# Alternating the array's halves in the half-array products of two recurrences

## The chip, the cores and the metric

The kernel runs on one core of a Trainium2 chip. The metric is device time in microseconds; the kernel before takes 3214.45 us (median of three runs, 3214.08 to 3216.48). TensorE is called PE below, with its weight loads as PEld; VectorE is DVE, ScalarE ACT, GpSimd POOL, SyncE SP.

## The reference

One block of a hybrid model over 2048 tokens of width 1024, in front of which 256 context tokens are scanned. Four branches (a gated convolution, a recurrence with a decay per channel, a Fourier mix, a recurrence with one decay per head) are gated and summed, and a hierarchical mixture of 32 experts follows. Both recurrences are this scan, run in both directions over four heads of 64 channels:

```python
def step(state, inp):
    qc, kc, vc, gc = inp
    cum = jnp.cumsum(gc, axis=-2)
    rel = cum[..., :, None, :] - cum[..., None, :, :]
    decay = jnp.exp(jnp.where(incl, rel, -jnp.inf))
    ...
    out = (jnp.einsum('bhts,bhse->bhte', scores, vc)
           + jnp.einsum('bhtd,bhde->bhte', qc * jnp.exp(cum), state))
    last = cum[..., -1:, :]
    state = (jnp.exp(last[..., 0, :])[..., None] * state
             + jnp.einsum('bhsd,bhse->bhde', kc * jnp.exp(last - cum), vc))
    return state, out
```

## The kernel before

The kernel is written in the tile framework: the order of the instructions on each engine is not the order of the code but is planned when the kernel is built, from the dependencies, the pools' buffers and assumed durations. Each engine then takes its instructions strictly in that order.

Stages, by the trace: modulation and norms, then projections (to 570 us); the first recurrence `hgrn` (576 to 908 us) beside the second half's projections; the second recurrence `ssm` (its preparation from 908, its products from 985 to 1266 us) beside the gates of the second half of the tokens; the Fourier branch (to about 1400 us) beside the rest of these gates; the gated sum of the branches (1465 to 2025 us); router and experts (to 3100 us); the weighted sum. Projections and gates are products of 128x128 weights with 512 or 256 columns in three parts (L1339 to L1341, tile `ps_mm`). They depend on no recurrence and are planned between the recurrences' instructions; below they are the fillers.

`hgrn` goes over four segments of 512 tokens, and two pairs of heads in each: eight passes. The two heads of a pair lie on partitions 0 to 63 and 64 to 127, so a product that contracts over one head's channels uses half of the array's rows. A pass computes scores without decay (L123) and then those of seven levels with blocks of 1, 2, 4 up to 64 tokens (L137). Such a group is four products of the first head and then four of the second, each head's in a bank `pa` of its own (tag `sc`, two banks), from which ACT (L124) or DVE (`copy_predicated`, L139) takes them into `ST`. DVE then multiplies `QP` by the level's decay (L143), the moving operand of the next group, and `K2` (L144), from which ACT makes the next level's `km` (L132). After the last level the states are advanced (L54, L59, L67) and the outputs `po` are summed in one bank (L156, L158, L159): for each of four chunks and two heads one product of values and scores (all 128 rows, 64 columns of the array), and two with the states that enter from the left and the right (64 rows, 64 columns). A square on ACT (L161), a product with ones (L163), a root on ACT (L165) and a reciprocal on DVE (L166) norm them.

`ssm` computes a state per chunk of 64 tokens in `d_state` (L311: two products on half of the rows, chunks alternate between the halves), backward over all chunks and then forward; per segment scores of two groups on half of the rows each (L393); and per 128 tokens and head one product with the scores (L413) and one for each of two chunks with the entering state (L417), 64 columns of the array each, heads alternating between the column halves.

All these products are fp32, and the profile shows each as two matmul records.

Of the kernel before, what the change touches and what calls it, by code (L numbers as in the profile page):

```python
# [21 lines left out]
def mix(base, off, n, w, B):  # L22
    """halves of blocks of 2B: the left ones of part 0, the right ones of part 1 (parts w apart)"""
    return ap_of(base, off, [[2 * B, n // (2 * B)], [w + B, 2], [1, B]])


def hgrn(G, tc, khm, FT, KT, QT, GT, V, YT, bufs=1):
    """FT, KT [2 dir, 2 panel][128, TA]; QT, GT [2 panel][128, T]; V [18][128, 256]; YT [2][128, T]"""
    nc = tc.nc
    SEG = 512  # L30
    with tc.tile_pool(reuse_waits="tile", name="hst", bufs=1) as st, tc.tile_pool(reuse_waits="tile", name="hw", bufs=bufs) as wp, \
# [17 lines left out]
        def states(ks, tot, v, hp, n, cs, S, src, dst):  # L49
            """ks [128, n] decayed keys, tot [128, n/128]; cs: chunks in order; S[:, hp, dst(c)] from S[:, hp, src(c)]"""  # L50
# [38 lines left out]
        # context: the final states of both directions start the scans  # L89
# [3 lines left out]
        # backward states: SB[c] enters chunk c from the right  # L93
# [5 lines left out]
        for sg in range(4):  # L99
# [3 lines left out]
            for hp in range(2):  # L103
# [13 lines left out]
                nc.vector.tensor_add(km, K2[:, 0], K2[:, 1])  # L117
                for h in range(2):
                    r = slice(h * 64, h * 64 + 64)
                    pa = G.psum("sc")  # L120
                    for c in range(4):
                        s = slice(c * 128, c * 128 + 128)
                        nc.tensor.matmul(pa[:, s], km[r, s], q[r, s], start=True, stop=True)  # L123
                    nc.scalar.copy(ST[:, h].rearrange("p c t -> p (c t)"), pa)  # L124
# [3 lines left out]
                while B < 128:  # L128
# [3 lines left out]
                    nc.scalar.copy(kmv, mix(K2, 0, n, n, B))  # L132
                    for h in range(2):
                        r = slice(h * 64, h * 64 + 64)
                        pa = G.psum("sc")
                        for c in range(4):
                            nc.tensor.matmul(pa[:, c * 128:c * 128 + 128], km[r, c * 128:c * 128 + 128],  # L137
                                             mix(QP[r], c * 128, 128, n, B), start=True, stop=True)
                        nc.vector.copy_predicated(ST[:, h], hmask[:, lev].unsqueeze(1).to_broadcast([128, 4, 128]),  # L139
                                                  pa.rearrange("p (c t) -> p c t", t=128))  # L140
# [11 lines left out]
                for c in range(4):  # L152
                    s = slice(c * 128, c * 128 + 128)
                    for h in range(2):
                        r = slice(h * 64, h * 64 + 64)
                        nc.tensor.matmul(po[r, s], v[:, c, hp * 128 + h * 64:hp * 128 + h * 64 + 64], ST[:, h, c, :],  # L156
                                         start=True, stop=False)
                        nc.tensor.matmul(po[r, s], SF[r, hp, c0 + c], QP[r, 1, s], start=False, stop=False)  # L158
                        nc.tensor.matmul(po[r, s], SB[r, hp, c0 + c], QP[r, 0, s], start=False, stop=True)  # L159
# [15 lines left out]
def ssm(G, tc, dtr, XR, ZT, XC, XB, cumD, ecumD, elD, SBd, YT):  # L175
    """dtr [128, 18, 8] raw steps (tokens on partitions); XR [4][128, TA] xs0 xs1 b c before the convolution; ZT [2][128, T];
    scratch in DRAM: XC [4][128, TA], XB [18][128, 384], cumD [2, 8, 18, 64], ecumD [8, TA], elD [8, 36], SBd [32][64, 256]"""
    nc = tc.nc
    NCH = TA // 64
    with tc.tile_pool(reuse_waits="tile", name="sst", bufs=1) as st:  # L180
        # ---- steps and cumulated logs
# [85 lines left out]
        with tc.tile_pool(reuse_waits="tile", name="sw", bufs=1) as wp, tc.tile_pool(reuse_waits="tile", name="ssp", bufs=2) as sp:  # L267
            # ---- convolution
# [37 lines left out]
            def d_state(xb, xw, c, d):  # L306
                i, r = c // 2, slice((c % 2) * 64, (c % 2) * 64 + 64)
                pd = G.psum("sc")
                o = slice(d * 64, d * 64 + 64)
                for g in range(2):  # L310
                    nc.tensor.matmul(pd[o, g * 128:g * 128 + 128], xb[r, i, 256 + g * 64:320 + g * 64],  # L311
                                     xw[r, i, g * 128:g * 128 + 128], start=True, stop=True)
                return pd[o, 0:256]
# [10 lines left out]
            # ---- context: final states; then the backward states of all chunks  # L324
            S = None
            xb, xw = seg_in(T, TC, 1)
            for c in (3, 2, 1, 0):
                S2 = sp.tile([128, 256], F32, name="Sb", bufs=3)
                step(S2, S, 32 + c, d_state(xb, xw, c, 1), 1)
                S = S2  # L330
            for sg in (3, 2, 1, 0):
                xb, xw = seg_in(sg * 512, 512, 1)
                for c in range(7, -1, -1):
                    ch = sg * 8 + c
                    nc.sync.dma_start(SBd[ch], S[64:128])
                    if ch:
                        S2 = sp.tile([128, 256], F32, name="Sb", bufs=3)
                        step(S2, S, ch, d_state(xb, xw, c, 1), 1)
                        S = S2
            S = None  # L340
            xb, xw = seg_in(T, TC, 0)
            for c in range(4):
                S2 = sp.tile([128, 256], F32, name="Sf", bufs=4)
                step(S2, S, 32 + c, d_state(xb, xw, c, 0), 0)
                S = S2
# [5 lines left out]
            for sg in range(4):  # L351
# [35 lines left out]
                PT = PTs[0]  # L387
                for g in range(2):
                    pa = G.psum("sc")
                    r = slice(g * 64, g * 64 + 64)  # L390
                    for i in range(4):
                        s = slice(i * 128, i * 128 + 128)
                        nc.tensor.matmul(pa[:, s], bT[r, s], cT[r, s], start=True, stop=True)  # L393
                    pv = pa.rearrange("p (i c t) -> p i c t", c=2, t=64)
# [5 lines left out]
                for i in range(4):  # L400
                    Sc = []
                    for c2 in range(2):
# [4 lines left out]
                        if ch < 31:  # L407
                            S2 = sp.tile([128, 256], F32, name="Sf", bufs=4)
                            step(S2, S, ch, d_state(xb, xw, c, 0), 0)
                            S = S2  # L410
                    for h in range(4):
                        g, o = h // 2, slice((h % 2) * 64, (h % 2) * 64 + 64)
                        nc.tensor.matmul(py[g][o, i * 128:i * 128 + 128], xb[:, i, h * 64:h * 64 + 64], PT[:, h, i],  # L413
                                         start=True, stop=False)
                        for c2 in range(2):
                            a = i * 128 + c2 * 64
                            nc.tensor.matmul(py[g][o, a:a + 64], Sc[c2][:, h * 64:h * 64 + 64], ec[:, h, a:a + 64],  # L417
                                             start=False, stop=c2 == 1)
# [19 lines left out]
def rnd12(a):  # L438
    """nearest float32 with 11 explicit mantissa bits"""
# [5 lines left out]
def dft_consts():  # L445
    """time: cos, sin of 2 pi t t'/2048, t' odd (512), 2 mod 4 (256), 4 mod 8 and 0 mod 8 (128, 130 with 1024);
    channels: cos, sin of 2 pi c c'/64 with the ortho scale, two groups on the diagonal"""
    def cs(n, tp):
        ph = (np.arange(n)[:, None] * np.asarray(tp)[None, :]) % 2048
        a = ph * (2 * np.pi / 2048)  # L450
        return np.stack([np.cos(a), np.sin(a)], 1).astype(np.float32)   # [t, 2, t']
    def split(a):
        hi = rnd12(a)
        return np.stack([hi, rnd12(a - hi)], 1)                      # [t, hi/lo, 2, t']
# [13 lines left out]
def fft(G, tc, U, YT, A):  # L468
    """U [16][128, 256] tokens on partitions; YT [2][128, T]"""
# [76 lines left out]
CAP = 2048          # a token picks an expert at most once  # L546
NSLOT = 2           # blocks per expert in the straight part: 128 tokens, then 64
FIT = 192
NONE = 1 << 20      # no assignment
RAW, PARTS = 9, 15  # panels of experts' weights on chip: as they come, in two parts  # L550
AHEAD = 6           # tiles loaded ahead in the last step
OVB = 32            # bound on the blocks beyond those


def ffn(tc, G, A, out, bcast, rsqrt, split, mm3, MT, MR, X1, FR, YB, mid):
# [9 lines left out]
    hl = rp.tile([128, 2, 2, N], BF, name="hl")             # (token + k T) / 64 + 1, and the rest  # L565
# [8 lines left out]
    def assign(dst_a, dst_r, v, t):  # L574
        """assignments and rows of tokens from table values v (-64: none)"""
# [6 lines left out]
    # ---------------- output projection, second norm, routing  # L582
    # its operands lie where the mixer's did
    wring = mid.wring
    with tc.tile_pool(reuse_waits="tile", name="wo", bufs=1, side="right") as wop, \
# [6 lines left out]
        wo = [y0, [[t[:, 2 * k:2 * k + 2] for t in w1] for k in range(4)]]      # columns, pair of chunks, part  # L592
# [78 lines left out]
        def route(p0, i0, M, lg):  # L671
            """the tiles of tokens i0 .. i0 + M, p0 tiles were before: weights, ranks among an expert's tokens, table"""
# [5 lines left out]
            def first_max(src, k, n):  # L678
                """maximum and the first place that has it, as 0/1"""
# [59 lines left out]
            # weights: the group's probability times the softmax over the two  # L739
# [12 lines left out]
        # in the order in which they come; a tile's logits stand between the next ones' products  # L752
# [3 lines left out]
        at, tiles = {}, {}              # what follows a half of a tile's products  # L756
# [29 lines left out]
    # ---------------- experts  # L786
# [4 lines left out]
    def unit(src, q=nc.sync, eng=nc.vector):  # L791
        """the two parts of a panel of an expert's weights"""
# [6 lines left out]
    class InTurn:  # L799
        """panels that are fetched when their turn comes, one at a time"""  # L800
# [762 lines left out]
```

## Time and profile before

| what | value |
|---|---|
| runs, median (lowest to highest) | 3214.45 us (3214.08 to 3216.48) |
| the profiled execution: span from the first to the last instruction | 3204.4 us |
| median less that span | 10.0 us |
| PE busy | 2935.5 us, 92% |
| weight loads busy | 2333.6 us, 73% |
| DVE busy | 1903.9 us, 59% |
| ACT busy | 1239.4 us, 39% |
| POOL busy | 856.6 us, 27% |
| mean granted TensorE clock | 0.962 |

No separate time of the profiled execution is given beside its span; 10 us is what the median of the runs has more. Busy time is the union of an engine's instructions; matmuls are pipelined and their ends are modelled, so two records can overlap in time without running beside each other, and the distance from one start to the next tells more than a duration. A granted clock of 1.00 is 2.4 GHz, 0.50 is 1.2 GHz. In a timeline, successive instructions of one line, tile and shape are merged into one row with their count.

### The profile page before, as it was taken

The numbers are of one execution on the slowest core, as the hardware profiler recorded it, in microseconds if no ns is written. First come the engines' busy times: TensorE is split into PE (matmuls) and PEld (weight loads), VectorE is DVE, ScalarE is ACT, GpSimd is POOL, SyncE is SP. The second block draws the span as 40 slices with busy tenths as digits, with TensorE's granted clock in tenths as the row PEclk, the third lists the DMA queues.
The fourth block names the chain that finished last, engine by engine and source line by source line (L and its number), as shares of the span: only waits on it lengthen the run. The fifth ranks groups of instructions, "written<-read, shape, count | busy, mean of one in ns | idle before, by whom it ended". The sixth has DMA issues, their size and how long they took to land. (4 is left out here: it accounts for less than half of the span.)

```text
span 3204.4 us, 40958 instructions
## 1 busy us (share of the span) xinstructions
PE 2935.5 (92%) x14805; PEld 2333.6 (73%) x14805; DVE 1903.9 (59%) x2956; ACT 1239.4 (39%) x1751; POOL 856.6 (27%) x589
## 2 busy tenths in 40 slices
PE   7998999999988999899999999999699999999950
PEld 4887887787766677677777777877577887778740
DVE  4524125877776568523334334566888768776758
ACT  5411132322236122132213212222577667776744
POOL 3300010000013112013334333000345544544435
PEclk8999999999998999999999999999799999999975
DMA  7636244422128476866336334432787888888884
GB/s 299 231 122 190 85 158 156 134 75 84 53 78 262 145 190 189 266 228 218 127 127 207 125 126 153 159 127 104 270 309 281 276 275 316 307 298 281 284 316 178
DMA packets 241878, 625.50 MB, mean 195 GB/s; under 512 B 27832, under 2 KB 75608, under 8 KB 237944
## 3 DMA queue, kind: packets, MB, share of 16 engines
q1 hardware_dynamic: 208784, 513.34, 47.1%
q0 software_dynamic: 32880, 109.38, 10.2%
q8 instruction: 126, 2.06, 0.3%
q14 instruction: 88, 0.72, 0.1%
HBM read 501.47 MB, written 129.27 MB: 197 GB/s over the span
## 5 line engine op out<-in xcount | busy, mean ns | idle before, releaser
L1196 DVE TENSOR_TENSOR mlo<-mraw,mhi 128x1024 fp32r<-128x1024 f32 x318 | 388.6, 1275 | 3.3 <-ACT mhi L1195 3.1
L1195 ACT CAST mhi<-mraw 128x1024 fp32r<-128x1024 f32 x384 | 387.0, 1053 | 7.1 <-DMA mraw<-e 6.8
L1339 PE MATMUL ps_mm<-hb1h,wlo 128*128 128x512 f32 x800 | 319.3, 399 | 10.3 <-ACT ev L1490 10.2
L1340 PE MATMUL ps_mm<-hb1l,whi 128*128 128x512 f32 x800 | 318.6, 398 | 0.0
L1341 PE MATMUL ps_mm<-hb1h,whi 128*128 128x512 f32 x800 | 318.3, 398 | 0.0
L1490 ACT ACTIVATE ev<-ps_mm 128x512 f32<-128x512 f32 x128 | 76.3, 598 | 594.4 <-PE ps_mm L1341 501.8
L1196 DVE TENSOR_TENSOR wlo<-wraw,whi 128x1024 fp32r<-128x1024 f32 x164 | 215.1, 1320 | 134.2 <-ACT whi L1195 132.1
L1339 PE MATMUL ps_mm<-hb0h,wlo 128*128 128x512 f32 x672 | 269.4, 401 | 6.3 <-DVE wlo L1196 6.3
L1340 PE MATMUL ps_mm<-hb0l,whi 128*128 128x512 f32 x672 | 269.3, 401 | 0.0
L1341 PE MATMUL ps_mm<-hb0h,whi 128*128 128x512 f32 x672 | 268.4, 399 | 0.0
L1540 POOL TENSOR_TENSOR macc<-macc,ev 128x512 f32<-128x512 f32 x96 | 167.3, 1743 | 309.5 <-DVE ev L1539 306.6
L1196 POOL TENSOR_TENSOR mlo<-mraw,mhi 128x1024 fp32r<-128x1024 f32 x66 | 209.9, 3196 | 136.4 <-ACT mhi L1195 125.8
L1195 ACT CAST whi<-wraw 128x1024 fp32r<-128x1024 f32 x176 | 182.2, 1045 | 152.8 <-PE ps_mm L1341 65.5
L1539 DVE TENSOR_TENSOR ev<-ev,ps_tr 128x512 f32<-128x512 f32 x96 | 65.8, 687 | 248.3 <-PE ps_tr L1341 244.0
L1339 PE MATMUL ps_mm<-mhi,xl 128*128 128x512 f32 x512 | 204.8, 400 | 0.1
L831 POOL DMA_INDIRECT xg<-d_FR,idx x48 | 129.3, 2695 | 270.8 <-PE ps_tr L848 221.6
L1341 PE MATMUL ps_mm<-mhi,xh 128*128 128x512 f32 x512 | 201.1, 393 | 0.3
L1340 PE MATMUL ps_mm<-mlo,xh 128*128 128x512 f32 x512 | 200.8, 392 | 0.3
L1339 PEld LDWEIGHTS ps_mm<-hb1h,wlo 128*128 128x128 f32 x800 | 151.5, 189 | 44.9 <-ACT ev L1490 11.0
L1340 PEld LDWEIGHTS ps_mm<-hb1l,whi 128*128 128x128 f32 x800 | 151.4, 189 | 33.5 <-issue 3.0
L1341 PEld LDWEIGHTS ps_mm<-hb1h,whi 128*128 128x128 f32 x800 | 151.2, 189 | 33.8 <-issue 2.7
L1339 PEld LDWEIGHTS ps_mm<-hb0h,wlo 128*128 128x128 f32 x672 | 127.8, 190 | 35.2 <-DVE wlo L1196 7.1
(605 smaller groups left out, 6618.4 us busy)
## 6 DMA issues: line engine op xcount, KB each, us to landing
mraw<-e SPq DMA_DIRECT2D x372, 512.0 KB
wraw<-wg SPq DMA_DIRECT2D x80, 512.0 KB
wraw<-wt SPq DMA_DIRECT2D x40, 512.0 KB
aw<-adaw SPq DMA_DIRECT2D x64, 256.0 KB
d_GS<-ev SPq DMA_DIRECT2D x64, 256.0 KB
ev<-d_GS POOLq DMA_DIRECT2D x64, 256.0 KB, 4.7
yk<-d_YB SPq DMA_DIRECT2D x32, 512.0 KB
wraw<-wg POOLq DMA_DIRECT2D x24, 512.0 KB, 4.4
```

Source lines behind the costliest of these rows:

```text
L831: nc.gpsimd.indirect_dma_start(out=xg, out_offset=None, in_=FR, in_offset=bass.IndirectOffsetOnAxis(ap=idx_ap, axis=0), bounds_check=T - 1 ...
L1195: nc.scalar.copy(hi, raw)
L1196: eng.tensor_sub(lo, raw, hi.bitcast(F32))
L1339: nc.tensor.matmul(ps, wl, xh, start=start and n == 0, stop=False)
L1340: nc.tensor.matmul(ps, wh, xl, start=False, stop=False)
L1341: nc.tensor.matmul(ps, wh, xh, start=False, stop=stop and n == len(ks) - 1)
L1490: nc.scalar.activation(g, ps, AF.Sigmoid)
L1539: nc.vector.tensor_mul(g, g, ps)
L1540: nc.gpsimd.tensor_add(acc, acc, g)
```

## The change

In both recurrences the products on half of the array are written so that the halves take turns, and each half has its own bank:

- the groups L123 and L137 of `hgrn` take both banks first and then go chunk by chunk, one head after the other; the two copies out of the banks follow the eight products;
- `po` is summed in three runs of one shape each: the entering states of the first head, then values and scores of both heads in turn, then the entering states of the second head; the flags that start a sum move with it;
- `d_state` becomes `d_states`, which makes the states of two chunks, in turn, in two banks;
- the scores L393 take both banks and go group by group in turn; of the outputs first the four heads' products with the scores are issued and then those with the entering states, the heads in turn.

No product, copy or transfer is added or removed.

```diff
+                pa = [G.psum("sc") for _ in range(2)]
+                for c, h in product(range(4), range(2)):
+                    r, s = slice(h * 64, h * 64 + 64), slice(c * 128, c * 128 + 128)
+                    nc.tensor.matmul(pa[h][:, s], km[r, s], q[r, s], start=True, stop=True)
                 for h in range(2):
-                    r = slice(h * 64, h * 64 + 64)
-                    pa = G.psum("sc")
-                    for c in range(4):
-                        s = slice(c * 128, c * 128 + 128)
-                        nc.tensor.matmul(pa[:, s], km[r, s], q[r, s], start=True, stop=True)
-                    nc.scalar.copy(ST[:, h].rearrange("p c t -> p (c t)"), pa)
+                    nc.scalar.copy(ST[:, h].rearrange("p c t -> p (c t)"), pa[h])
...
+                    pa = [G.psum("sc") for _ in range(2)]
+                    for c, h in product(range(4), range(2)):
+                        r, s = slice(h * 64, h * 64 + 64), slice(c * 128, c * 128 + 128)
+                        nc.tensor.matmul(pa[h][:, s], km[r, s], mix(QP[r], c * 128, 128, n, B), start=True, stop=True)
                     for h in range(2):
-                        r = slice(h * 64, h * 64 + 64)
-                        pa = G.psum("sc")
-                        for c in range(4):
-                            nc.tensor.matmul(pa[:, c * 128:c * 128 + 128], km[r, c * 128:c * 128 + 128],
-                                             mix(QP[r], c * 128, 128, n, B), start=True, stop=True)
                         nc.vector.copy_predicated(ST[:, h], hmask[:, lev].unsqueeze(1).to_broadcast([128, 4, 128]),
-                                                  pa.rearrange("p (c t) -> p c t", t=128))
+                                                  pa[h].rearrange("p (c t) -> p c t", t=128))
...
-                for c in range(4):
-                    s = slice(c * 128, c * 128 + 128)
-                    for h in range(2):
-                        r = slice(h * 64, h * 64 + 64)
-                        nc.tensor.matmul(po[r, s], v[:, c, hp * 128 + h * 64:hp * 128 + h * 64 + 64], ST[:, h, c, :],
-                                         start=True, stop=False)
-                        nc.tensor.matmul(po[r, s], SF[r, hp, c0 + c], QP[r, 1, s], start=False, stop=False)
-                        nc.tensor.matmul(po[r, s], SB[r, hp, c0 + c], QP[r, 0, s], start=False, stop=True)
+                def entering(h):
+                    r = slice(h * 64, h * 64 + 64)
+                    for c in range(4):
+                        s = slice(c * 128, c * 128 + 128)
+                        nc.tensor.matmul(po[r, s], SF[r, hp, c0 + c], QP[r, 1, s], start=h == 0 and c == 0, stop=False)
+                        nc.tensor.matmul(po[r, s], SB[r, hp, c0 + c], QP[r, 0, s], start=False, stop=h == 1 and c == 3)
+                entering(0)
+                for c, h in product(range(4), range(2)):
+                    r, s = slice(h * 64, h * 64 + 64), slice(c * 128, c * 128 + 128)
+                    nc.tensor.matmul(po[r, s], v[:, c, hp * 128 + h * 64:hp * 128 + h * 64 + 64], ST[:, h, c, :],
+                                     start=h == 1 and c == 0, stop=h == 0 and c == 3)
+                entering(1)
...
-            def d_state(xb, xw, c, d):
-                i, r = c // 2, slice((c % 2) * 64, (c % 2) * 64 + 64)
-                pd = G.psum("sc")
+            def d_states(xb, xw, cs, d):
                 o = slice(d * 64, d * 64 + 64)
-                for g in range(2):
-                    nc.tensor.matmul(pd[o, g * 128:g * 128 + 128], xb[r, i, 256 + g * 64:320 + g * 64],
+                pd = {c: G.psum("sc") for c in cs}
+                for g, c in product(range(2), cs):
+                    i, r = c // 2, slice((c % 2) * 64, (c % 2) * 64 + 64)
+                    nc.tensor.matmul(pd[c][o, g * 128:g * 128 + 128], xb[r, i, 256 + g * 64:320 + g * 64],
                                      xw[r, i, g * 128:g * 128 + 128], start=True, stop=True)
-                return pd[o, 0:256]
+                return {c: p[o, 0:256] for c, p in pd.items()}
...
                     for h in range(4):
-                        g, o = h // 2, slice((h % 2) * 64, (h % 2) * 64 + 64)
-                        nc.tensor.matmul(py[g][o, i * 128:i * 128 + 128], xb[:, i, h * 64:h * 64 + 64], PT[:, h, i],
+                        p, o = at(h)
+                        nc.tensor.matmul(p[o, i * 128:i * 128 + 128], xb[:, i, h * 64:h * 64 + 64], PT[:, h, i],
                                          start=True, stop=False)
-                        for c2 in range(2):
-                            a = i * 128 + c2 * 64
-                            nc.tensor.matmul(py[g][o, a:a + 64], Sc[c2][:, h * 64:h * 64 + 64], ec[:, h, a:a + 64],
-                                             start=False, stop=c2 == 1)
+                    for c2, h in product(range(2), range(4)):
+                        p, o = at(h)
+                        a = i * 128 + c2 * 64
+                        nc.tensor.matmul(p[o, a:a + 64], Sc[c2][:, h * 64:h * 64 + 64], ec[:, h, a:a + 64],
+                                         start=False, stop=c2 == 1)
```

The callers of `d_states` ask for two chunks at a time, at odd chunks on the way back and at even ones on the way forward. The order on every engine is planned anew; it is the same up to the first level group (579 us) and again from the gated sum of the branches on. PE has 14,965 rows with the changed kernel as before; SP and POOL have the same rows in an order that differs by a few places; ACT has 52 table loads, 48 before; one copy of `ev` goes from DVE to ACT or back with the balance. In the rows below, the tiles are named output<-moving operand, stationary operand; `ps_sc` are the banks of scores, `ps_tr` those of sums and transposes.

PE, two steady levels of the fourth pass of `hgrn`, before:

```order
L137 MATMUL ps_sc<-QP,km 128x128 x8
L1340 MATMUL ps_mm<-hb0l,whi 128x512
L1341 MATMUL ps_mm<-hb0h,whi 128x512
L1339 MATMUL ps_mm<-hb0h,wlo 128x512
L1340 MATMUL ps_mm<-hb0l,whi 128x512
L1341 MATMUL ps_mm<-hb0h,whi 128x512
L1339 MATMUL ps_mm<-hb0h,wlo 128x512
L1340 MATMUL ps_mm<-hb0l,whi 128x512
L137 MATMUL ps_sc<-QP,km 128x128 x8
```

The same place with the changed kernel:

```order
L137 MATMUL ps_sc<-QP,km 128x128 x8
L1356 MATMUL ps_mm<-hb1h,wlo 128x512
L1357 MATMUL ps_mm<-hb1l,whi 128x512
L1358 MATMUL ps_mm<-hb1h,whi 128x512
L1356 MATMUL ps_mm<-hb1h,wlo 128x512
L1357 MATMUL ps_mm<-hb1l,whi 128x512
L1358 MATMUL ps_mm<-hb1h,whi 128x512
L1356 MATMUL ps_mm<-hb0h,wlo 128x512
L1357 MATMUL ps_mm<-hb0l,whi 128x512
L1358 MATMUL ps_mm<-hb0h,whi 128x512
L137 MATMUL ps_sc<-QP,km 128x128 x8
```

Between two groups there are now nine fillers instead of seven.

PE, the last level and the start of the output block of the same pass, before:

```order
L137 MATMUL ps_sc<-QP,km 128x128 x8
L59 MATMUL ps_tr<-hv,kt 128x128 x3
L156 MATMUL ps_tr<-ST,hv 64x128
L1340 MATMUL ps_mm<-hb1l,whi 128x512
L1341 MATMUL ps_mm<-hb1h,whi 128x512
L1339 MATMUL ps_mm<-hb1h,wlo 128x512
L158 MATMUL ps_tr<-QP,SF 64x128
L159 MATMUL ps_tr<-QP,SB 64x128
L156 MATMUL ps_tr<-ST,hv 64x128
L158 MATMUL ps_tr<-QP,SF 64x128
```

The middle of the output block with the changed kernel (L157 and L158 are now the entering states, L164 values and scores):

```order
L157 MATMUL ps_tr<-QP,SF 64x128
L158 MATMUL ps_tr<-QP,SB 64x128
L164 MATMUL ps_tr<-ST,hv 64x128 x8
L157 MATMUL ps_tr<-QP,SF 64x128
L158 MATMUL ps_tr<-QP,SB 64x128
```

The 24 products of a block are now three runs of eight of one shape each, with no filler inside.

PE, the backward states of `ssm`, before:

```order
L311 MATMUL ps_sc<-xw,xb 64x128 x2
L1340 MATMUL ps_mm<-hb1l,whi 128x512
L1341 MATMUL ps_mm<-hb1h,whi 128x512
L1339 MATMUL ps_mm<-hb1h,wlo 128x512
L1340 MATMUL ps_mm<-hb1l,whi 128x512
L311 MATMUL ps_sc<-xw,xb 64x128 x2
```

The same place with the changed kernel:

```order
L319 MATMUL ps_sc<-xw,xb 64x128 x2
L1357 MATMUL ps_mm<-hb0l,whi 128x512
L1358 MATMUL ps_mm<-hb0h,whi 128x512
L1356 MATMUL ps_mm<-hb0h,wlo 128x512
L1357 MATMUL ps_mm<-hb0l,whi 128x512
L319 MATMUL ps_sc<-xw,xb 64x128 x2
```

Here nothing moved: each pair of products is still one chunk's.

## Rows read from the trace of the kernel before

**Rows 1.** Busy us by stage: PE, PEld, DVE, ACT, POOL, clock, DMA share, GB/s

```profile
576.00:908.00 332.00, 329.42 (x2165) 257.90 (x2164) 242.24 (x408) 89.02 (x140) 12.09 (x9) 1.00 0.25 78
...
985.00:1266.00 281.00, 262.22 (x1457) 192.45 (x1457) 188.80 (x257) 86.43 (x109) 64.85 (x64) 0.96 0.66 192
1465.00:2025.00 560.00, 542.44 (x2368) 443.45 (x2366) 227.18 (x238) 131.50 (x164) 212.27 (x176) 1.00 0.46 149
```

**Rows 2.** Timeline of PE, levels of the fifth pass: start, us, instruction

```profile
745.49 2.34 PE L137 MATMUL ps_sc<-QP,km 64*128 64x128 f32 x16
...
753.07 1.82 PE L137 MATMUL ps_sc<-QP,km 64*128 64x128 f32 x16
...
760.54 1.71 PE L137 MATMUL ps_sc<-QP,km 64*128 64x128 f32 x16
...
762.75 0.40 PE L1340 MATMUL ps_mm<-hb1l,whi 128*128 128x512 f32 x1
762.98 0.40 PE L1341 MATMUL ps_mm<-hb1h,whi 128*128 128x512 f32 x1
...
764.00 1.71 PE L137 MATMUL ps_sc<-QP,km 64*128 64x128 f32 x16
```

**Rows 3.** Timeline of PE: one half's scores in the second recurrence, whole and in part

```profile
1139.01 1.16 PE L393 MATMUL ps_sc<-cT,bT 64*128 64x128 f32 x8
...
1141.44 0.71 PE L393 MATMUL ps_sc<-cT,bT 64*128 64x128 f32 x4
```

**Rows 4.** Timeline of PE: states of one chunk, and of two in both halves

```profile
1128.67 0.65 PE L311 MATMUL ps_sc<-xw,xb 64*64 64x128 f32 x4
...
1130.40 0.66 PE L311 MATMUL ps_sc<-xw,xb 64*64 64x128 f32 x8
```

**Rows 5.** Timeline of PE: one round of the output block

```profile
775.19 0.43 PE L156 MATMUL ps_tr<-ST,hv 128*64 128x128 f32 x2
775.55 0.43 PE L158 MATMUL ps_tr<-QP,SF 64*64 64x128 f32 x2
775.82 0.38 PE L159 MATMUL ps_tr<-QP,SB 64*64 64x128 f32 x2
776.13 0.43 PE L156 MATMUL ps_tr<-ST,hv 128*64 128x128 f32 x2
```

**Rows 6.** Timeline of PE: outputs of heads; first and last row of 28 records

```profile
1129.25 0.27 PE L417 MATMUL ps_tr<-ec,Sf 128*64 128x64 f32 x1
1129.26 0.32 PE L413 MATMUL ps_tr<-PT,xb 128*64 128x128 f32 x1
...
1136.19 0.22 PE L417 MATMUL ps_tr<-ec,Sf 128*64 128x64 f32 x1
...
1137.85 0.65 PE L311 MATMUL ps_sc<-xw,xb 64*64 64x128 f32 x4
```

**Rows 7.** Timelines of DVE and PE: a level's copies and multiply, and the next group

```profile
637.78 0.69 DVE L143 TENSOR_TENSOR QP<-QP,tot 128x512 f32<-128x512 f32 x1
638.61 0.34 PE L137 MATMUL ps_sc<-QP,km 64*128 64x128 f32 x1
...
761.73 1.37 DVE L139 COPY_PREDICATED ST<-hmask,ps_sc 128x512 f32<-128x512 int32 x2 [0.81 <-PE ps_sc L137]
762.98 0.68 DVE L143 TENSOR_TENSOR QP<-QP,tot 128x512 f32<-128x512 f32 x1
```

**Rows 8.** Timelines of DVE and ACT behind the output block

```profile
741.54 1.22 DVE L114 TENSOR_TENSOR QP<-F,hq 128x1024 f32<-128x1024 f32 x1 [4.79 <-PE ps_tr L159]
744.25 3.35 DVE L166 RECIPROCAL rr<-rr 128x512 f32<-128x512 f32 x1 [0.89 <-ACT rr L165]
744.85 1.14 ACT L124 COPY ST<-ps_sc 128x512 f32<-128x512 f32 x2
752.31 0.71 ACT L132 COPY km<-K 128x512 f32<-128x512 f32 x1 [0.63 <-DVE K L144]
```

**Rows 9.** Waits of PE, 908 to 1266 us: us in total, times, longest

```profile
PE ps_mm L1339 <- ACT ev L1490: 10.2, 2, 6.0
```

More of the change, by code (lines that the diff above doesn't have):

```diff
@@ L1 @@
+from itertools import product
 import numpy as np
@@ L327, in ssm @@
             for c in (3, 2, 1, 0):
+                if c % 2:
+                    pd = d_states(xb, xw, (c, c - 1), 1)
                 S2 = sp.tile([128, 256], F32, name="Sb", bufs=3)
-                step(S2, S, 32 + c, d_state(xb, xw, c, 1), 1)
+                step(S2, S, 32 + c, pd[c], 1)
                 S = S2
@@ L335, in ssm @@
                     nc.sync.dma_start(SBd[ch], S[64:128])
+                    if c % 2:
+                        pd = d_states(xb, xw, (c, c - 1) if ch > 1 else (c,), 1)
                     if ch:
                         S2 = sp.tile([128, 256], F32, name="Sb", bufs=3)
-                        step(S2, S, ch, d_state(xb, xw, c, 1), 1)
+                        step(S2, S, ch, pd[c], 1)
                         S = S2
@@ L342, in ssm @@
             for c in range(4):
+                if c % 2 == 0:
+                    pd = d_states(xb, xw, (c, c + 1), 0)
                 S2 = sp.tile([128, 256], F32, name="Sf", bufs=4)
-                step(S2, S, 32 + c, d_state(xb, xw, c, 0), 0)
+                step(S2, S, 32 + c, pd[c], 0)
                 S = S2
@@ L387, in ssm @@
                 PT = PTs[0]
+                pa = [G.psum("sc") for _ in range(2)]
+                for i, g in product(range(4), range(2)):
+                    r, s = slice(g * 64, g * 64 + 64), slice(i * 128, i * 128 + 128)
+                    nc.tensor.matmul(pa[g][:, s], bT[r, s], cT[r, s], start=True, stop=True)
                 for g in range(2):
[L389 to L394, printed above, removed]
+                    pv = pa[g].rearrange("p (i c t) -> p i c t", c=2, t=64)
                     for c2 in range(2):
@@ L401, in ssm @@
                     Sc = []
+                    pd = d_states(xb, xw, (i * 2, i * 2 + 1) if sg * 4 + i < 15 else (i * 2,), 0)
                     for c2 in range(2):
@@ L408, in ssm @@
                             S2 = sp.tile([128, 256], F32, name="Sf", bufs=4)
-                            step(S2, S, ch, d_state(xb, xw, c, 0), 0)
+                            step(S2, S, ch, pd[c], 0)
                             S = S2
+                    at = lambda h: (py[h // 2], slice((h % 2) * 64, (h % 2) * 64 + 64))
                     for h in range(4):
-                        g, o = h // 2, slice((h % 2) * 64, (h % 2) * 64 + 64)
-                        nc.tensor.matmul(py[g][o, i * 128:i * 128 + 128], xb[:, i, h * 64:h * 64 + 64], PT[:, h, i],
+                        p, o = at(h)
+                        nc.tensor.matmul(p[o, i * 128:i * 128 + 128], xb[:, i, h * 64:h * 64 + 64], PT[:, h, i],
                                          start=True, stop=False)
-                        for c2 in range(2):
-                            a = i * 128 + c2 * 64
-                            nc.tensor.matmul(py[g][o, a:a + 64], Sc[c2][:, h * 64:h * 64 + 64], ec[:, h, a:a + 64],
-                                             start=False, stop=c2 == 1)
+                    for c2, h in product(range(2), range(4)):
[3 more added lines that the diff above has]
+                                         start=False, stop=c2 == 1)
                 for g in range(2):
```

## The prediction

> **What bounds the kernel now.** I read the busy times by stage first. While the first recurrence runs (576 to 908 us) TensorE (PE) is busy 329.4 of 332 us at the full clock, and it is also the fullest engine from 985 to 1266 us (262 of 281) and from 1465 to 2025 us (542 of 560) [rows 1]. So between 576 and 2025 us the time is PE's work plus its idle time: projections and gates, which no recurrence waits for at once, fill PE between the recurrence's steps, and whatever is saved is filled by gates that would have come later. After the last Fourier product 257 gate products of 512 columns are still left before the merge (272 in the new order, both counted there), some 60 us at 0.23 us each [rows 2], so the fillers do not run out.
>
> Second, PE's timeline in steady levels: a group of 8 products (16 records, each product being two), seven fillers, the next group, 3.46 us from group to group [rows 2]. Third, the timeline of single groups, for what halves do beside each other. One half's 8 records take 1.16 us [rows 3]; 16 take 1.71 [rows 2]. Four records alone take 0.71 in another place [rows 3], so four more cost 0.45, 0.11 each; 16 in a row would take 1.16 + 8 x 0.11 = 2.05. The missing 0.34 is three records of the second half that ran beside the first. In the other recurrence 8 records of two chunks, which lie in different halves, take 0.66, as 4 of one chunk take 0.65 [rows 4]. So halves with a bank each do run together; today only where one half's run meets the other's.
>
> **Levels (L123, L137).** 64 groups, one for the undecayed scores and seven levels for each of eight passes. Alternated, both halves take the time of one: 1.71 becomes 1.16, 0.55 saved. 48 such groups save 26.4 us. The level with blocks of 2 takes 1.82 and that with blocks of 1 takes 2.34, since their moving operand is strided [rows 2]; in the same ratio 0.59 and 0.75, times eight each, 10.7. Sum **37 us**; bounds 0 (no pairing beyond today's) and 37. I take 37: the paired rate is seen in rows 4, if over 8 records and not 16.
>
> The Trainium skill speaks against this (TensorE: Matmul & The Clock Gate, LDWEIGHTS): a weight load costs its columns at 1.2 GHz, whatever rows it fills, which is 107 ns here. Were loads to pass one at a time, 16 would take 1.71 us paired or not, and this term would be 0. The trace does not agree: by rows 4 eight products' loads and streams pass in the time of four.
>
> **Output block (L156, L158, L159).** Each of eight rounds of six records takes 0.94 us: two records of the 128x64 shape, four of 64x64, two changes of shape [rows 5]. From the first L158 to L159 are 0.27 and on to the next L156 0.31, so records follow 0.11 apart and a change costs 0.20 - 0.11 before it and 0.05 behind it, 0.14. Now all 16 records of the entering states of one half stand together, then 16 of the scores, then the other half's 16. The score records alternate between the array's column halves, and rows 6 show that this pairs too: L413 of one head starts 0.01 us after L417 of another. The block falls from 8 x 0.94 = 7.52 to 32 x 0.11 + 8 x 0.11 + 3 x 0.14 = 4.8. Three fillers inside the old block cost two more changes, 0.3. Eight times 3.0 is **24 us**; 17 if columns don't pair.
>
> **Second recurrence.** The scores (L393) come as eight halves that hold PE about 1.1 us each [rows 3]; four pairs instead, **4 us** (bound 0). Head outputs (L413, L417): 28 records, 20 of 64 columns and 8 of 128, take 1.66 us [rows 6]. At half of 0.11 for 64 columns they are 1.98 one after another and 0.99 paired; 384 records are 13.7 times as many, 9 us, of which I take **8** since the new order still breaks runs (bounds 0 and 9). Chunk states (L311): the order still places each chunk's two products alone, 52 rows of x2 before and after, because a bank frees one at a time. **0**, bounds 0 and 3.
>
> PE's work: 37 + 24 + 4 + 8 = **73 us** less.
>
> **What comes back as waiting.** The order fills freed time: a steady level has nine fillers, not seven, and takes 3.46 - 0.55 + 0.46 = 3.37 us on PE. What PE must wait for: the first copy starts 1.19 after the group, which the change leaves, since the first half ran at full rate already; 1.25 to the multiply, 0.68 for it [rows 7], and 0.14 from one such multiply's end to PE's start [rows 7]. That is 3.26, so PE comes later by 0.1 and nothing waits: price 0, and up to 5 us if the copies slip.
>
> Behind the output block it is different. DVE starts the next pass when L159 ends, having waited up to 4.8 us for it; then the norm, a 3.35 us reciprocal that blocks DVE, the first level's multiplies and ACT's copy lead to the group at 753.07: 11.5 us from 741.54 [rows 2, 8]. Today PE fills exactly this. In the new order PE has 24 fillers there, not 27 (0.7), and groups shorter by 0.55 and 0.75: 9.5 us. It would wait 2.0 us a pass. In three passes the key multiply moves ahead of the last products on DVE, which shortens the chain by about its ACT copy, 0.7. I take 1.5, eight times: **12 us** back (bounds 0 and 16). Before the first level PE waits for ACT's two copies out of the banks: they take 1.14 [rows 8] from the group's end at 1.2, so they end some 2.4 us after it started, and PE is there at 2.0 (its 1.3 and three fillers); **3 us**. From 985 to 1266 us PE idles 19 us today for DVE, ACT and transfers [rows 1]; it now comes 12 us sooner there; I take **3**, bounds 0 and 12. Four more ACT table loads, some stores and weight fetches a few rows later on SP's and POOL's queues, with no transfer more or less: hidden beside PE, ACT being far from full, or in those bounds.
>
> No clock cost: from 1465 to 2025 PE idles 17.6 us in short waits and holds 1.00 [rows 1].
>
> **Sum.** 73 - 18 = 55 us. The profiled span is 3204.4, the median of the runs 3214.45; the 10 us around the span are not touched. Forecast **3159 us**.
>
> **Rivals.**
> A. The waits do not come, because the chain behind the block shortens with the block. For it: today the same places fit with almost no wait. Against: the rows of that chain are DVE's and ACT's own durations. 3214 - 73 = 3141.
> B. Pairing over long runs holds half the time. The overlap of today is three records deep, not more. Levels give 19, the rest as forecast, and waits as forecast: 3177.
> C. No pairing beyond today's; only changes of shape go. 13 of 15 inner changes a block, 13 x 0.14 + 0.3, eight times: 17 us. 3197. Rows 4 and 6 are against it. The weight-load rule of the Trainium skill (TensorE: Matmul & The Clock Gate, LDWEIGHTS), taken as a queue of loads, would give this.
> D. Slower: gate panels come too late. PE's largest single wait in these stages is 6.0 us, for the evacuation of gates [rows 9]. PE uses panels faster, and on POOL's queue the eighth panel's fetch stands behind seven stores of the convolution, not three, and the thirteenth behind 37, not 30. From ten late panels on, at 6.0 each, 60 us are lost and more than the 55 gained; twelve give 3214 - 55 + 72 = 3231. Against it: only two such waits exist today.
> E. The change does nothing: PE's freed time all turns into waits in the recurrence's chain. For it: that chain is as long as PE's work to 0.1 us a level. Against: the order puts 43 more fillers of 512 columns (427 to 470) into the first recurrence. 3214.
>
> **Chances.** Forecast 0.46, A 0.22, B 0.15, C 0.08, D 0.05, E 0.04. For 8 in 10 the range must take in the forecast with its bounds (waits 3 to 33, so 3144 to 3174), most of A and all of B: from 3132 (A with the 4 us that the upper bounds leave and 5 of today's 19 us of waits) to 3190 (B with 13 of its 15 us of further waits). This kernel can be told from no change at about 0.2%, 6 us. Faster: the forecast, A, B and C, 0.91; within: E, 0.04; slower: D, 0.05.
>
> **What would show it.** Right: L137 x16 rows of 1.16 us instead of 1.71; an output block of 4.8 us with one run of 16 score records; the first recurrence ending near 872 us instead of 908 (61 - 10 for more fillers - 15 of waits); PE's idle time there near 17 us instead of 2.6, most of it before the group with blocks of 2; the merge starting near 1410 us instead of 1465, and the stages behind it of the same length. Wrong: groups over 1.4 us (B or C), a first copy that starts later than 1.19 after its group, or PE idle from 908 to 1465 us grown by more than 20 us (D).

## The result, and the profile after

The changed kernel takes 3166.41 us (median of four runs, 3165.99 to 3167.94) where the kernel before, on the same chip, takes 3215.47: a ratio of 0.986 with a 95% interval of [0.983, 0.990]: faster, by less than 2%. A second set of runs (e5, below) gave 0.989 [0.985, 0.993], with a median of 3175.7 us. By these ratios 35 to 44 us were won; 55 were forecast, and both medians lie in the range.

The busy time by stage of the changed kernel, in the columns of [rows 1]: the first recurrence, the stretch behind it, the products of the second, and the gated sum.

```profile
571.60:881.00 309.40, 286.44 (x2194) 228.78 (x2194) 242.29 (x406) 92.59 (x143) 11.99 (x10) 0.97 0.27 86
881.00:956.00 75.00, 54.63 (x256) 43.41 (x256) 60.34 (x125) 37.94 (x41) 12.89 (x17) 0.84 0.34 108
956.00:1232.80 276.80, 255.98 (x1449) 185.60 (x1449) 187.37 (x258) 87.20 (x110) 60.70 (x65) 0.92 0.67 198
1438.60:1994.00 555.40, 538.79 (x2355) 440.22 (x2353) 226.78 (x236) 131.45 (x164) 211.37 (x175) 1.00 0.44 149
```

The first recurrence is 22 us shorter, not 36; PE idles 23 us there (309.40 less 286.44), not 17; and the granted clock, 1.00 before, falls below it. PE's timeline in the fifth pass, with one row of ACT's, against [rows 2] and [rows 5]:

```profile
722.98 1.16 PE L122 MATMUL ps_sc<-hq,km 64*128 64x128 f32 x16
...
724.17 1.08 ACT L124 COPY ST<-ps_sc 128x512 f32<-128x512 f32 x2
...
724.97 1.91 PE L137 MATMUL ps_sc<-QP,km 64*128 64x128 f32 x16
...
731.72 1.23 PE L137 MATMUL ps_sc<-QP,km 64*128 64x128 f32 x16 [0.99 <-DVE QP L143]
...
735.47 1.16 PE L137 MATMUL ps_sc<-QP,km 64*128 64x128 f32 x16 [0.25 <-DVE QP L143]
...
753.15 0.43 PE L157 MATMUL ps_tr<-QP,SF 64*64 64x128 f32 x2
...
755.04 1.09 PE L164 MATMUL ps_tr<-ST,hv 128*64 128x128 f32 x16
...
757.95 0.50 PE L1356 MATMUL ps_mm<-hb1h,wlo 128*128 128x512 f32 x1
```

Sixteen records take 1.16 us, the group with blocks of 2 takes 1.23, and the output block 757.95 - 753.15 = 4.80. These are the forecast values. The group with blocks of 1 takes 1.91, where 1.59 were forecast: its second half starts only at 725.30, since the second bank is free when ACT's second copy has ended (724.17 + 1.08 = 725.25). The eighth pass is another matter:

```profile
851.87 0.40 PE L1358 MATMUL ps_mm<-hb1h,whi 128*128 128x512 f32 x1
853.45 1.16 PE L137 MATMUL ps_sc<-QP,km 64*128 64x128 f32 x16 [1.18 <-DVE QP L143]
857.10 1.87 PE L137 MATMUL ps_sc<-QP,km 64*128 64x128 f32 x16 [2.49 <-DVE QP L143]
860.99 2.08 PE L137 MATMUL ps_sc<-QP,km 64*128 64x128 f32 x16 [2.02 <-DVE QP L143]
...
869.81 0.43 PE L157 MATMUL ps_tr<-QP,SF 64*64 64x128 f32 x2 [2.77 <-DVE QP L143]
...
872.30 1.97 PE L164 MATMUL ps_tr<-ST,hv 128*64 128x128 f32 x16
...
878.62 2.08 PE L170 MATMUL ps_tr<-o,c_kblk 128*128 128x512 f32 x2 [0.75 <-ACT o L168]
893.23 0.79 PE L1356 MATMUL ps_mm<-hb0h,wlo 128*128 128x512 f32 x1 [12.53 <-DVE wlo L1213]
```

From 851.87 to 893.23 us no filler stands between the recurrence's steps. PE waits for each level's multiply; then groups of the same form take 2.08 instead of 1.16 and L164 1.97 instead of 1.09. The granted clock tells why (stretches of 10 us: length, PE busy with its count, clock, DMA share, GB/s):

```profile
840.00:850.00 10.00, 9.98 (x58) 1.00 0.25 96
850.00:860.00 10.00, 5.09 (x51) 0.87 0.22 79
860.00:870.00 10.00, 5.56 (x46) 0.79 0.00 0
870.00:880.00 10.00, 9.25 (x50) 0.55 0.01 2
880.00:890.00 10.00, 0.70 (x1) 0.50 0.11 37
```

PE is busy for half of the 20 us from 850 to 870, and the clock falls from 1.00 (2.4 GHz) to 0.50 (1.2 GHz) from 857 to 864 us and again from 871 to 898. The first gate product afterwards waits 12.53 us for a weight panel's low part. On ACT the panel's high part is cast only here:

```profile
887.83 1.05 ACT L1212 CAST whi<-wraw 128x1024 fp32r<-128x1024 f32 x1 [4.11 <-DVE hy L176]
```

It waits for `hy`, the last tile that the recurrence writes. The same product before waits 4.90 us for its panel, behind 39 fillers that stand after the recurrence's last product:

```profile
920.22 0.70 PE L1339 MATMUL ps_mm<-hb0h,wlo 128*128 128x512 f32 x1 [4.90 <-DVE wlo L1196]
...
921.14 0.63 PE L1341 MATMUL ps_mm<-hb0h,whi 128*128 128x512 f32 x1
921.57 0.63 PE L1339 MATMUL ps_mm<-hb0h,wlo 128*128 128x512 f32 x1
```

The panel is the third of the gates'. Every third one (`wx if j % 3 == 2`) is not in the ring of weight buffers but in a pool `wx`, which is opened when the first recurrence closes and lies in its memory. So up to the recurrence's end only two gate panels can be had, however many gates are left later: up to then the trace has four sums of gates, two for each panel.

Pass by pass (from one undecayed score group to the next, the last to the end of L163 or L170; idle is the time in which no product runs, fillers those of 512 columns that the order has there):

| pass | 1 | 2 | 3 | 4 | 5 | 6 | 7 | 8 |
|---|---|---|---|---|---|---|---|---|
| before, us | 41.8 | 43.4 | 41.1 | 40.5 | 40.1 | 41.1 | 40.3 | 41.2 |
| after, us | 39.2 | 37.2 | 38.0 | 37.0 | 37.2 | 36.9 | 37.5 | 46.2 |
| before, idle | 0.3 | 0.1 | 0.1 | 0.1 | 0.1 | 0.4 | 0.1 | 0.9 |
| after, idle | 2.9 | 0.6 | 1.5 | 1.5 | 1.4 | 1.3 | 2.6 | 10.8 |
| before, fillers | 64 | 22 | 22 | 65 | 63 | 67 | 64 | 64 |
| after, fillers | 69 | 17 | 42 | 74 | 75 | 74 | 71 | 48 |

Seven passes are 25 us shorter together although they hold 55 more fillers; the eighth is 5 longer, with 16 fillers fewer. That makes 39 more fillers in all; the prediction counted 43.

### The profile page after: what moved, and what is told of

It is laid out like the page before. It is cut to its first block, busy times and chain, and to the rows that moved or that the text cites. A ratio compares the mean times of both kernels' runs of the same rounds, so it can differ in the third digit from the quotient of the medians.

```text
span 3166.2 us, 40956 instructions
## 1 busy us (share of the span) xinstructions
PE 2876.7 (91%) x14805; PEld 2291.8 (72%) x14805; DVE 1893.4 (60%) x2957; ACT 1243.8 (39%) x1754; POOL 853.5 (27%) x589
## 5 line engine op out<-in xcount | busy, mean ns | idle before, releaser
L1213 DVE TENSOR_TENSOR mlo<-mraw,mhi 128x1024 fp32r<-128x1024 f32 x318 | 378.2, 1242 | 2.8 <-ACT mhi L1212 2.2
```

Of the source, the lines that this page charges most:

```text
L1213: eng.tensor_sub(lo, raw, hi.bitcast(F32))
```

## The experiments

**e1, e5: the two kernels again.** No edit. Expected:

> The kernel before, unchanged, timed against itself: it shows how far two sets of runs of the same kernel lie apart, and its profile is a second one of the same work. In the profile read ahead of the change the first recurrence starts at 576.8 us, in that of the changed kernel at 571.6 us, though the order of the instructions is the same up to there; and from the router to the end the first takes 1180 us and the second 1172. Theory 1: these 13 us are scatter between executions; this run then has a start within 571 to 577 us, and a ratio of 1.000 within 0.003. Rival: the profile read before was an ordinary one, and this one shows the same 576.8 and 1180 to 1 us.

> The changed kernel, unchanged, timed again with more rounds beside the kernel before, since four runs left an interval of 0.983 to 0.990. Theory 1 (gates run out in the eighth pass of the first recurrence): the time is 30 to 50 us below before, and the profile shows again seven passes of 37 to 39 us and an eighth of 46 us, at a granted clock that falls to 0.50. Rival (the long eighth pass was an accident of one execution): the eighth pass takes 37 to 39 us here.

Measured: e1 has 1.000 [0.998, 1.002]. Its recurrence starts at 573.5 us, and the stretch from there to the gated sum's first accumulation takes 913 us, where the profile read before has 894. e5 has 0.989 [0.985, 0.993], the same stretch takes 872 us as in the first profile of the changed kernel (872), and its eighth pass takes 47.1 us. So the long eighth pass belongs to the kernel. The differences ahead of the recurrence are scatter: with the changed kernel it starts at 571.6 us in the first profile and at 578.3 in e5's. From its start to the gated sum the profile read before is the shortest of three of that kernel (e7's, below, has 906 us).

**e2, e3, e4: the parts alone.** e2 is the first two hunks of the diff on the kernel before, e3 the third, e4 the rest. Expected:

> The kernel before, with only the score groups of the first recurrence alternated (both banks first, then chunk by chunk one head after the other). Theory 1: the groups alone bring the full 1.71 to 1.16 us, some 34 us of PE work, and the plan fills it with gates until they run out in the eighth pass (51 fillers of 512 columns there, 70 to 76 in the four passes before), so that PE idles some 8 us in its levels and the time falls by about 20 to 25 us, to 3190. Rival (waits of each pass, not of the last): PE idles 1.5 us and more in every pass, and the last pass is like the others; then the time falls by 34 - 12 = 22 as well, but with the idle time spread.

> The kernel before, with only the output block of the first recurrence in three runs of one shape. Theory 1: the block takes 4.8 to 5 us instead of 7.5, 18 to 21 us of PE work in eight blocks; the plan has 65 to 69 fillers in each full pass, the last one included, so little of it is lost to waits: 12 to 18 us less, 3200. Rival (the chain behind the block sets the pass): PE idles 1.5 us and more ahead of the group with blocks of 2, and under 8 us are won.

> The kernel before, with only the second recurrence changed (states of two chunks together, scores and head outputs alternated). Theory 1: head outputs take 18 instead of 28 us of PE, scores 8 instead of 9.5, states 40 instead of 36.5, so some 8 us of PE work go; with PE's waits there for DVE, ACT and transfers unchanged the time falls by 4 to 8 us. Rival: the waits grow by what is saved, and the time is the same within 3 us.

Measured: e2 0.999 [0.996, 1.001], e3 0.997 [0.995, 0.999], e4 0.996 [0.993, 0.998]. The largest part alone, 34 us of PE work, wins nothing that can be told, less than either theory expected. Its levels are shortened (L137 takes 71.3 us in all, 101.5 before). Its idle time shows both theories at once, 12 us spread over the first seven passes and 8.3 in the eighth, which takes 49.9 us:

```profile
883.68 1.16 PE L137 MATMUL ps_sc<-QP,km 64*128 64x128 f32 x16 [3.32 <-DVE QP L143]
...
905.90 2.08 PE L163 MATMUL ps_tr<-o,c_kblk 128*128 128x512 f32 x2 [0.75 <-ACT o L161]
920.50 0.80 PE L1339 MATMUL ps_mm<-hb0h,wlo 128*128 128x512 f32 x1 [12.53 <-DVE wlo L1196]
```

The recurrence takes 333 us with it (575.1 to 908.0), where before takes 330 and 331 (e1): all that seven passes gained, some 5 to 7 us while they took in 52 more fillers, the eighth gives back, and the same 12.53 us wait follows. e3, with PE idle 1.2 us in its eighth pass and 0.1 to 0.6 in the others, has a recurrence 20 us shorter; its ratio shows about 10 of them (4 to 16 by the interval), less than the 12 to 18 expected, and what became of the rest was not settled. e4's ratio shows some 14 us, but its interval (7 to 21) takes in the 8 us that were expected at most.

**e6, e7, e11: the third gate panel in the ring.**

```diff
-            w = wpanel(A["wg"][j], wx if j % 3 == 2 else None, q=nc.gpsimd if len(bs) == 2 else nc.sync,
+            w = wpanel(A["wg"][j], wx if j % 3 == 2 and j > 2 else None, q=nc.gpsimd if len(bs) == 2 else nc.sync,
...
```

> The changed kernel, with the third gate panel in the ring of two buffers that the first two use, and no longer in the memory that comes free when the first recurrence ends. Theory 1: that memory is why the gates ran out; the plan now puts 88 fillers of 512 columns into the eighth pass instead of 48. PE idles 1 to 2 us there, not 10.8, the clock stays at 1.00 and the 12.5 us wait behind the last norm is gone; some 20 us against the changed kernel, to a ratio of about 0.978 to 0.984. Rival: PE idles for DVE's multiplies in every pass and the gates are only shifted, so the later stages have fewer of them and wait longer; then the time is that of the changed kernel within 5 us.

> The kernel before, with the third gate panel in the ring in the same way. There the gates last until 4.9 us before the panel comes, and the eighth pass is as long as the others. Theory 1: only that wait and a short drop of the clock behind it are won, 0 to 8 us. Rival (the ring is better by itself, whatever the pairing): about 20 us are won here too.

> The changed kernel with the third gate panel in the ring once more, since it is the fastest of all and its interval (0.979 to 0.986) only just leaves that of the changed kernel (0.985 to 0.993). Theory 1: 0.979 to 0.986 again, with an eighth pass of 39 us. Rival: its lead was the scatter of one set of runs, and it comes out at 0.987 to 0.991 like the changed kernel.

Measured: e6, on the changed kernel, 0.983 [0.979, 0.986], and again as e11 0.982 [0.979, 0.985]; e7, on the kernel before, 1.001 [0.999, 1.003]. So the ring wins time that can be told only where the groups are paired. The eighth pass of e6 takes 39.4 us with 88 fillers and 0.9 us idle, at full clock:

```profile
842.00:852.00 10.00, 9.77 (x62) 1.00 0.23 89
852.00:862.00 10.00, 9.76 (x75) 1.00 0.16 57
862.00:872.00 10.00, 10.00 (x80) 1.00 0.13 50
872.00:882.00 10.00, 10.00 (x63) 1.00 0.00 0
```

The stretch from the recurrence's start to the gated sum takes 855 and 847 us, against 872. This version beats both kernels. Its interval touches that of the changed kernel, but beside each other, in e5 and e6, the changed kernel's six runs take 3163 to 3185 us and those with the ring 3145 to 3165; in e11's set the ring has 3153.7 us where before takes 3212.5.

What the ring gives back is the eighth pass: its idle time and its clock, and 40 more fillers in it. The wait of 12.53 us is gone, but PE's idle time from the recurrence's end to the gated sum's first accumulation stays at 57 us (56.7 in e6, 57.2 in the changed kernel), since other waits grow there. The two largest groups (waits of PE in e6 from 571 to 1440 us: us in total, times, longest) are

```profile
PE ps_tr L269 <- ACT R L251: 11.3, 1, 11.3
PE ps_mm L1356 <- DVE wlo L1213: 10.4, 2, 7.5
```

In the changed kernel L269 waits 8.0 us, and later panels 3.5 beside the 12.5.

**e9: the paired groups alone, with the ring.** e2 and e7 put together:

> The kernel before, with the alternated score groups alone and the third gate panel in the ring. By themselves the groups gave a ratio of 0.999 and the ring 1.001. Theory 1 (the groups' gain was lost in the eighth pass, for want of gates): the plan has 79 fillers of 512 columns in that pass instead of 51; it takes 40 us instead of 49.9 without a drop of the clock, the wait of 12.5 us behind it goes, and the ratio is 0.991 to 0.996. Rival (the groups win nothing because each pass waits for DVE's multiplies): 0.998 to 1.001, as the sum of the two.

Measured: 0.992 [0.989, 0.994], an eighth pass of 39.9 us with 79 fillers and 0.6 us idle. Two edits that win nothing alone win some 27 us together. That settles where most of the groups' gain had gone.

**e8: the same banks and copies, the halves in succession.**

```diff
-                for c, h in product(range(4), range(2)):
+                for h, c in product(range(2), range(4)):
```

for L122 and, in the same way, L137.

> The changed kernel, with the score groups of the first recurrence written as both banks first and then the first head's four products and the second's, the two copies behind: banks and copies as in the change, only the order of the eight products undone. Theory 1 (alternation makes the pairing): the groups take 1.71 us again, and a ratio of about 0.99, that of the output block and the second recurrence together. Rival (the second bank and the copies behind the group make it): the groups take 1.16 us.

Measured: 0.992 [0.989, 0.995], and a group of

```profile
758.11 1.71 PE L137 MATMUL ps_sc<-QP,km 64*128 64x128 f32 x16
```

So, with a bank for each half, it is the order of the eight products alone that makes 1.16 of 1.71. Whether alternation would do so in a single bank was not tried. The ratio of e8 lies beside that of the changed kernel in the same set (e5, 0.989 [0.985, 0.993]): without the ring the alternated groups win nothing that can be told here either.

**e10: the column halves in succession.** e6 with

```diff
-                for c, h in product(range(4), range(2)):
+                for h, c in product((1, 0), range(4)):
```

in the output block's run L164.

> The changed kernel with the third gate panel in the ring, and in the output block's run of values and scores the second head's four products first and then the first head's: still one run of one shape, but the column halves no longer take turns. The block of 48 records takes 4.80 us with them. Theory 1 (column halves run beside each other): the 16 records take 16 steps of 0.11 us instead of 8, so the block takes 5.5 to 5.7 us. Rival (only the changes of shape cost): it stays at 4.8 us within 0.1.

Measured in one execution: the run takes 1.58 us instead of 1.09,

```profile
759.59 1.58 PE L164 MATMUL ps_tr<-ST,hv 128*64 128x128 f32 x16
```

and the block 5.29 instead of 4.80. Column halves do run beside each other; the gain is 0.49 us, not the 0.7 to 0.9 expected, because in succession some of it is there already, as in the levels.

## Why the prediction was right, and where it failed

**Levels: 37 us forecast, 33.6 found.** L123 and L137 took 13.7 + 101.5 us of PE; as L122 and L137 they take 9.3 + 72.3. What lacks is the groups with blocks of 1, which take 1.90 to 1.92 us in five passes instead of 1.59, and two groups at half the clock in the eighth. e8 and the change have the same sixteen loads and differ by 0.55 us: loads on different rows of the array do not wait for each other here. With it rivals B and C fall. The Trainium skill (TensorE: Matmul & The Clock Gate, LDWEIGHTS) gives the price of one weight load by its columns, by an estimate from its figure 107 ns for 128. The 0.11 us from record to record within one half [rows 3] agree with it. That sixteen such loads would queue, to an estimate of 1.71 us, was the prediction's reading in rival C; this section of the Trainium skill does not state it, and so did not speak against the change.

**Output block: 24 us forecast.** [rows 5] give a round; the whole block of before takes 8.4 us with its three fillers. It takes 4.80 in seven passes, as forecast, and 8.8 in the eighth, at a granted clock of 0.50 from 871 us on. e10 shows that columns pair, the part that the lower bound of 17 left open.

**Second recurrence: 4 + 8 + 0 forecast.** The head outputs gave 7 to 10: from start to start L413 and L417 take 27.8 us, L429 and L434 18.1 in the changed kernel and 21 in e4 and e6. A run of heads reads

```profile
1107.17 0.44 PE L429 MATMUL ps_tr<-PT,xb 128*64 128x128 f32 x4
1107.44 0.64 PE L434 MATMUL ps_tr<-ec,Sf 128*64 128x64 f32 x16
```

The scores (L405) gave 1.5, not 4: three of four segments still issue one half's four products and then the other's, probably since the two halves' banks come free one at a time; the prediction saw this for the states and not here. The states show no change that can be told: start to start they take 36.5 us in the profile read before and 40.9 in e1's, 39.8 and 39.0 in those of the changed kernel.

**Waits: 18 us forecast; the sum of seven passes came right in part by luck.** There idle time grows by 10.6 us (forecast 12 + 3 for eight, so 13). In four of the seven the largest single wait is the one named, before the group with blocks of 2 (0.99 above). But this wait comes in five passes, at 0.8 to 1.0 us, 4.7 in all where 1.5 in each pass were forecast. The steady levels, priced at 0, wait 0.2 to 1.3 us for their multiply in some passes and not in others, 5.2 in all: the margin of 0.1 us a level was too thin to be called none. The wait for ACT's two copies (3 us forecast) is there as the longer groups with blocks of 1, 0.3 us in five passes. With waits that come rival A falls, and with 25 us won in seven passes rival E.

**The step that failed: "so the fillers do not run out".** It counted the gates left before the merge. What decides is which of them can be had by then: two panels, until the recurrence's memory is free. The plan moved fillers ahead into shorter levels, as forecast, and by the eighth pass they were spent. That cost 9.9 us more idle time in that pass than before, and the wait behind it is 7.6 us longer (12.53 against 4.90 before). The second step that failed hangs on it: **"No clock cost"**. The prediction took it from a stretch where PE idles in short waits; here PE was left busy for half of 20 us, the clock fell to 0.50, and a block of 4.80 us took 8.8. And [rows 1] had a stretch with a clock of 0.96, 985 to 1266 us, which the prediction passed over. It has 0.92 in the changed kernel, but 0.92 too in e1's profile of the kernel before, so that part of the clock's cost is not shown to be the change's. Rival D named late panels, but another cause: the queue's order, where here it is memory. With the shortage taken away (e6, e11) the kernel wins 55 to 57 us by the ratios, close to the forecast of 55, though not term by term, as the sum shows.

**The sum.** From the recurrence's first group to the gated sum's first accumulation, PE busy time and the rest (length, PE busy, clock, DMA share, GB/s), before:

```profile
576.80:1470.90 894.10, 841.45 (x4734) 0.98 0.51 159
```

after:

```profile
571.60:1443.50 871.90, 792.08 (x4738) 0.94 0.51 163
```

PE's busy time falls by 49 us and idle time grows by 27. But busy time is not work: at a clock of 0.50 successive fillers start 0.43 us apart, not 0.23 (behind the wait at 920.22 above), and PE is busy at 0.50 for 33 us of this stretch before and for 72 us after. Counting busy time at 0.50 as 0.23/0.43 of work gives an estimate of what the work is at full clock, and of what the clock adds. All profiles of the same kernel agree on the work to 3 us, though not on the rest (means, us):

| the same stretch | before, e1, e7 | after, e5 | e6, e11 |
|---|---|---|---|
| length | 904 | 872 | 851 |
| PE's work at full clock, estimate | 825 | 760 | 762 |
| added by the clock of 0.50, estimate | 21 | 31 | 17 |
| idle | 58 | 81 | 71 |

So the work falls by some 65 us where 73 were forecast: the second recurrence and the levels gave less. Idle time grows by some 23 where 18 were forecast, and the clock adds some 10 where nothing was, though single profiles overlap there (16 to 32 before, 29 to 34 after). That makes a stretch 32 us shorter, where the runs show 35 to 44 us; the single profiles of before lie between 894 and 913 us. With the ring the work is as in the changed kernel, and what it wins is idle time and clock.

The term for what lies around the span was wrong as well: this profiled execution takes 3167.94 us around a span of 3166.2, so the 10 us were not a fixed part of the time. And 0.2% was too fine: the intervals reach 0.2 to 0.4% to either side.

## What to carry to other kernels

Products on different halves of the array run beside each other where neighbours in the order lie in different halves; a second bank alone brings nothing (1.71 us in e8). Work that is to fill freed time must be counted where it is ready, panel by panel and buffer by buffer, not in total: the last pass before a pool closes is the place to look. When a sound part wins nothing, find the pass that gives its gain back before undoing it. And before busy times of two profiles are compared, the time at half the clock has to be told from work.

## What was not expected of the hardware

The column halves pair about as well as the row halves do, which the prediction had taken from two rows alone: sixteen records of 128 rows and 64 columns take 1.09 us alternated and 1.58 in succession, against 1.16 and 1.71 for sixteen records of 64 rows and 128 columns. And the scatter of this kernel is wide: the runs of the kernel before beside e2 lie between 3193 and 3224 us.
